# Two layers of a hybrid decoder: turning matmul results through a DRAM scratch on GpSimd's queue

## The chip, the cores and the metric

One core of one Trainium2 chip. The metric is the device time of one execution, in microseconds. Inputs are float32 and are laid out before the launch, features on the partitions.

## What is computed

Two layers on a sequence of 256 tokens with 2048 features. Every layer adds a mixer and then a gated MLP to the residual stream, each behind an RMS norm.

```
for l in range(2):
    h = rms_norm(x, mix_norm[l])
    x = x + (mixer_ab(h, ...) if l == 0 else mixer_c(h, ...))
    h = rms_norm(x, ffn_norm[l])
    x = x + conv_ffn(h, w_up[l], conv_w[l], conv_b[l], w_down[l])

conv_ffn: z = h @ w_up;  z = sum(conv_w[j] * z shifted by 2 - j tokens) + conv_b
          a, b = split(z);  return (silu(a) * b) @ w_down        # 5632 hidden
```

Mixer A is a causal gated MLP over chunks of 128 tokens, mixer B a gated linear recurrence with 8 heads, both with one output projection. Mixer C is attention with 16 heads, a forgetting gate, normalised q and k and an output gate.

## The kernel before

**Matmuls.** Each float32 weight and activation is split into a rounded part and a rest (`wh`, `wl` for weights; the two halves of a tile of 512 columns for activations), and three matmuls replace one: high by high, high by low, low by high. The weights are moved through the array in tiles of 128x1024 (two k-tiles of 128 rows by 512 output columns): a DMA on SyncE's queue (`weights`, L195), a cast on ScalarE (`wh`, L206), a subtraction on VectorE (`wl`, L211), then 12 matmuls of 512 columns. One such group is a *tick*. Buffers: four of `w` and three each of `wh` and `wl`; in the FFN every other group uses a second pool with two of each. Results stand in PSUM with tokens on the partitions, in two banks of 128 tokens; there are four banks for projections.

**Turning.** The next step needs features on the partitions. So a result of 256 tokens by 512 features, a *piece*, is evacuated by ScalarE to `z`, transposed in blocks of 32x32 by VectorE into `tmp` (`transposed`, L308), and moved to its place across partitions by DMAs (L314): 16 transfers of 32 KB per piece, eight on SyncE's queue and eight on GpSimd's. In the last piece of all, ScalarE's queue takes a share. There are 80 pieces. In the turned tile two tokens lie side by side, token t and token t + 128, and readers use a strided view (`turned`, `natural`).

**Order.** Generators hold the work around the matmuls; `tick()` advances them before each weight group. A reader of a piece begins `LAG` = 6 ticks after the piece (L315 ff. and `after`), the last piece of a layer `LAST` = 7 ticks. The tile framework then orders the instructions of each engine by its own estimate of durations, so the place of a reader in an engine's queue comes from that, with waits on semaphores where data is late.

**Pairs.** Where a layer's last pieces become the next layer's input, `project_pair` runs two accumulations at once: k-tiles 0 to 11 (`JOIN` = 12) of the first and then of the second, then tiles 12 to 15 of the first and of the second. The two pieces then end two ticks apart. The pair is used for the output projections (`output`) and at the start of each FFN.

**Other places that the change touches.** `conv` makes one ScalarE instruction and two on VectorE (L989, L990) per feature tile of 128. `forget` sends the gate row sums of mixer C to DRAM (`cd`, L806) and reads them back to all partitions in one transfer of 2 MB (`cb`, L807). `orow` is a broadcast read of 512 KB on GpSimd's queue (L541). The final pieces of the FFN go through `add_y`; the sums of its last piece (L158) stand before the sum of the last output tile (L1077) on VectorE.

Of the kernel before, what the change touches and what calls it, by code (L numbers as in the profile page):

```python
# [15 lines left out]
P = 128  # L16
# [9 lines left out]
LAG = 6  # L26
LAST = 7
WAIT = 2
JOIN = 12
EPS = 1e-6  # L30
# [23 lines left out]
def tile_trunk(ctx: ExitStack, tc: tile.TileContext, x, pp_d, cst_d, mlev_d, msk_d,  # L54
# [10 lines left out]

    count = [0]
# [18 lines left out]
    SC.dma_start(pp[:, 0:C_FFN], pp_d[:, 0:C_FFN])  # L85
# [24 lines left out]
    def turned(ap):  # L110

        return view(ap, 0, (1, 2), (2, P))

# [191 lines left out]
    def transposed(src, tmp, dst, queues=None):  # L305

        for T in range(2):
            V.transpose(tmp.rearrange("p (b m i t) -> p b m i t", b=4, m=4, t=2)[:, :, :, :, T],  # L308
                        src(T).rearrange("p (m b j) -> p b m j", m=4, b=4))
        n = 2 * BLK  # L310
        for a in range(4):
            for b in range(4):
                qs = queues or (nc.sync, nc.gpsimd)
                qs[(a + b) % len(qs)].dma_start(dst[BLK * b:BLK * (b + 1), :, a * n:(a + 1) * n],  # L314
                                  tmp[BLK * a:BLK * (a + 1), b * 4 * n:(b + 1) * 4 * n]  # L315
                                  .rearrange("p (m r) -> p m r", m=4))
# [83 lines left out]
    def add_four(q, ps, z, tmp, dst, nxt):  # L400
        for T in range(2):
            SC.activation(z[:, T], ps[T], AF.Copy)
        transposed(lambda T: z[:, T], tmp, dst)

        def rest():
            for i in range(4):
                m = 4 * q + i
                sum_in(xT[m], xT[m], dst[:, i], ALU.add)
                nxt.feed(m)
                if q < 3 or i % 2:  # L410
                    yield
            if q == 3:
                for _ in range(WAIT):
                    yield
                yield from nxt.finish_tok()

        after(LAST if q == 3 else LAG, rest())


    def mixer_ab(norm):  # L420
# [64 lines left out]
        for g in range(2):  # L485
            for T in range(2):
                i = (2 * g + T) * 4
                j = hp.tile([P, 512], F32, tag="smk", name=nm("junk"), bufs=1)
                sumsq(ss[:, i:i + 4], gv[g][:, T], j)
        rsq(ss[:, 0:2 * NH], ss[:, 0:2 * NH], P)  # L490
        for g in range(2):
            for T in range(2):
                i = (2 * g + T) * 4
                v4 = gv[g][:, T].rearrange("p (h d) -> p h d", d=P)
                V.tensor_tensor(v4, v4, ss[:, i:i + 4].unsqueeze(2).to_broadcast([P, 4, P]), ALU.mult)
# [14 lines left out]
        def mixes():  # L510
            yield
            yield
            yield
            for h in range(NH):
                mix(h)
                yield
# [21 lines left out]
        od = dp.tile([NH, P], F32, tag="od", name="od")  # L538
        orow = hp.tile([P, NH * P], F32, tag="orow", name="orow")
        nc.gpsimd.dma_start(od.rearrange("h p -> p h"), omlb)  # L540
# [3 lines left out]
        def turn(w4, late=False, use=None):  # L544
# [8 lines left out]
            t = t.rearrange("p (m t) -> p m t", m=4)  # L553
# [3 lines left out]
        def natural(z):  # L557
            return view(z, 0, (1, 2), (2, P))

        lf, kq, pair = [], [], []  # L560

        def gates(h, z):
# [5 lines left out]
            act_in(l.rearrange("p (t n) -> p t n", t=2), natural(z), AF.Sigmoid)  # L568
            act_in(t[:, 0::2], natural(z), AF.Sigmoid, scale=-1.0)
# [4 lines left out]
        def four_gates(j, z):  # L574
            for i in range(4):
                gates(4 * j + i, z[:, i])
                yield
# [6 lines left out]
        def hgrn(h):  # L584
# [68 lines left out]
            for T in range(2):  # L653
                SC.activation(itok[:, T, d0:d0 + P], op[:, T * P:(T + 1) * P], AF.Copy, scale=so[:, T:T + 1])
            left[0] -= 1

        def queries(j, z):
            while len(kq) < 4 * j + 4:
                yield
            for i in range(4):  # L660
                t = kq[4 * j + i]
                copy_in(view(t, 3 * P, (-2 * P, 2), (1, P)), natural(z[:, i]), AF.Copy)
# [33 lines left out]
        def gated(j, ps):  # L696
# [6 lines left out]
            t = hp.tile([P, 1024], F32, tag="QK", name=nm("turn"), bufs=2).rearrange("p (m t) -> p m t", m=4)  # L703
# [4 lines left out]
            gain = pp[:, C_ON:C_ON + 1]  # L708
            for i in range(4):
                y = yB[8 + 4 * j + i] = quad("yb")  # L710
                hi, lo = (y[:, c * S:(c + 1) * S].rearrange("p (t u n) -> p t u n", t=2, u=2) for c in range(2))
                copy_in(hi, view(t[:, i], 0, (2, 2), (1, 2), (4, P // 2)), AF.Copy, scale=gain)
                for u in range(2):
                    V.scalar_tensor_tensor(lo[:, :, u], view(t[:, i], u, (2, 2), (4, P // 2)), gain,
                                           hi[:, :, u].bitcast(F32), ALU.mult, ALU.subtract)
# [3 lines left out]
        def spatial(j, z):  # L719
# [3 lines left out]
            for i in range(4):  # L723
                b = 4 * j + i
                m = mg[b].rearrange("p (t n) -> p t n", t=2)
                V.tensor_tensor(m, m, natural(z[:, i]), ALU.mult)
                yB[b] = quad("ya")
                split(yB[b], mg[b], turn=True)
                yield
# [7 lines left out]
        for q, ps in enumerate(output(w_abo, yB, NH)):  # L737
# [3 lines left out]
            dst = dst.rearrange("p (m t) -> p m t", m=4)  # L741
# [5 lines left out]
    def mixer_c(norm):  # L747
# [38 lines left out]

        def forget():
# [19 lines left out]
            nc.gpsimd.dma_start(cb, cd.partition_broadcast(P))  # L807
# [9 lines left out]
        def attend(h, q, k, v, o):  # L817
# [4 lines left out]
            for j, (t, g) in enumerate(((q, gq), (k, pp[:, C_KN:C_KN + 1]))):  # L822
                copy_in(qk[:, j].rearrange("p (t n) -> p t n", t=2), turned(t[:, h % 4]), AF.Copy, scale=g)
# [45 lines left out]
        def heads(t):  # L869
            return flat(t).rearrange("p (m t) -> p m t", m=4)  # L870

        ready = [0]

        def turn(z, t):
# [10 lines left out]
            transposed(lambda T: z[:, T], flat(piece("tmp", 2)), heads(t))  # L885
# [4 lines left out]
        for g in range(CH // 4):  # L890
            qkv = []
            for j in range(3):
# [11 lines left out]
                if j < 2:  # L904
                    t = piece("turn", 4)
                    start(turn(z, t))
                    z = heads(t)
# [6 lines left out]
        def gate(q, z):  # L914
# [6 lines left out]
            t = piece("turn", 4)  # L921
            transposed(lambda T: z[:, T], flat(piece("tmp", 2)), heads(t))
# [3 lines left out]
            for i in range(4):  # L926
# [5 lines left out]
                src = view(heads(t)[:, i], 0, (2, 2), (1, 2), (4, P // 2))  # L932
                h, lo = (y[:, i_ * S:(i_ + 1) * S].rearrange("p (t u n) -> p t u n", t=2, u=2) for i_ in range(2))
# [13 lines left out]
        for q, ps in enumerate(output(w_co, yB)):  # L947
            add_four(q, ps, piece("z", 2), flat(piece("tmp", 2)), heads(piece("turn", 4)), nxt)
# [4 lines left out]
    def ffn(l, norm, last):  # L953
# [7 lines left out]
        def room():  # L961
            return (hp.tile([P, 1024], F32, tag="tmp", name=nm("tmp"), bufs=1),
                    hp.tile([P, 4, S], F32, tag="zt", name=nm("zt"), bufs=2))
# [17 lines left out]
        def conv(z, j, half):  # L981
# [6 lines left out]
            copy_in(c, z, AF.Identity, bias=pp[:, cb:cb + 1], scale=w(2))  # L988
            V.scalar_tensor_tensor(c[:, 1:], z[:, :S - 1], w(1), c[:, 1:], ALU.mult, ALU.add)  # L989
            V.scalar_tensor_tensor(c[:, 2:], z[:, :S - 2], w(0), c[:, 2:], ALU.mult, ALU.add)  # L990
            return c

        def up(j0):
# [4 lines left out]
            def gate():  # L998
                yield from ea
                for i in range(4):  # L1000
                    a = conv(za[:, i], j0 + i, 0)
# [7 lines left out]
            def fill():  # L1009
                yield from eb  # L1010
                for i in range(4):
                    b = conv(zb[:, i], HT + j0 + i, 1)
# [11 lines left out]
        def add_y(q, finish):  # L1024
# [5 lines left out]
            def rest():  # L1030
                for i in range(4):
                    m = 4 * q + i
                    r = sum_in(xT[m], xT[m], zt[:, i], ALU.add)
# [161 lines left out]
```

## Time and profile before

| | us |
|---|---|
| median of three runs | 2317.85 (2313.73 to 2318.16) |
| the profiled execution | 2317.44 |
| its span | 2315.7 |
| mean granted TensorE clock | 0.996 |

The span is one execution as the hardware profiler saw it; 1.7 us lie around it. PE is TensorE, PEld its weight loads, DVE VectorE, ACT ScalarE, POOL GpSimd, SP SyncE; SPq, ACTq and POOL's DMA lines are issues of transfers. L211 is line 211 of the kernel. In a row of the timeline stand start, length, engine, line, operation, output <- input, shapes and count, and in brackets the idle time of the engine before it with what ended it. In a group stand busy time and mean nanoseconds of one, then the idle time before. A row of the DMA issues has the count, the size of one and the median time from issue to landing.

### The profile page before, as it was taken

What the parts mean: (1) busy time and instruction counts of PE and PEld (TensorE: products, weight loads), DVE (VectorE), ACT (ScalarE), POOL (GpSimd) and SP (SyncE); (2) the same over time, 40 slices, a digit from 0 to 9 for tenths busy, and PEclk for the clock granted to TensorE, in tenths of its full rate; (3) what the DMA queues carried; (4) which work ended last, traced back from release to release, by engine and by line L of the source; (5) the groups of instructions that cost most, each with busy time, mean ns of one, the idle gap of its engine ahead of it and who ended that gap; (6) DMA issues with size and microseconds to landing.
All of it is one profiled execution on the core that took longest, in us unless ns stands there. A gap on an engine that the chain in (4) does not pass through costs nothing.

```text
span 2315.7 us, 31427 instructions
## 1 busy us (share of the span) xinstructions
PE 2292.7 (99%) x10370; PEld 1903.9 (82%) x10370; DVE 1557.9 (67%) x2369; ACT 1313.3 (57%) x1953; POOL 356.5 (15%) x661
## 2 busy tenths in 40 slices
PE   9999999999999999999989999999999999999999
PEld 7888887888888888888868888878888888888887
DVE  7788766777566657766756665657777467657666
ACT  7577655665455545654545556646655456456642
POOL 0101121122012002111211101121221022012102
PEclk9999999999999999999999999999999999999999
DMA  8755667777667657776666555767777677667765
GB/s 273 205 186 169 187 204 222 228 235 214 203 204 218 214 185 227 221 215 189 181 198 201 185 187 174 227 207 229 235 219 219 193 213 218 204 203 219 220 204 172
DMA packets 499204, 481.06 MB, mean 208 GB/s; under 512 B 116992, under 2 KB 468368, under 8 KB 498912
## 3 DMA queue, kind: packets, MB, share of 16 engines
q1 hardware_dynamic: 475344, 451.83, 62.5%
q0 software_dynamic: 21248, 23.69, 4.6%
q10 hardware_dynamic: 2448, 3.53, 0.5%
q8 instruction: 81, 1.33, 0.2%
q14 instruction: 83, 0.68, 0.1%
HBM read 434.85 MB, written 2.12 MB: 189 GB/s over the span
## 4 chain that ended last, share of the span: by engine, by line
PE 75%; DMA 2%; DVE 1%; SPq 1%; issue 0%; ACT 0%; DVEq 0%; ACTq 0%; POOLq 0%
PE pm L288 21%; PE pm L289 21%; PE pm L287 21%; PE pm L267 3%; PE pm L268 3%; PE pm L269 3%; SPq L314 1%; DMA zt<-tmp 1%; PE px L161 1%; PE px L770 1%; DMA turn<-tmp 0%; PE pm L771 0%; DVE wl L211 0%; DVE tmp L308 0%; PE px L164 0%
## 5 line engine op out<-in xcount | busy, mean ns | idle before, releaser
L211 DVE TENSOR_TENSOR wl<-w,wh 128x1024 fp32r<-128x1024 f32 (+1 forms) x812 | 986.7, 1218 | 655.6 <-ACT wh L206 650.0
L206 ACT ACTIVATE wh<-w 128x1024 fp32r<-128x1024 f32 (+1 forms) x812 | 854.6, 1054 | 796.3 <-PE pm L289 555.6
L288 PE MATMUL pm<-wl,a 128*128 128x512 f32 x1792 | 698.4, 390 | 2.9 <-DVE wl L211 2.9
L287 PE MATMUL pm<-wh,a 128*128 128x512 f32 x1792 | 701.0, 391 | 0.0
L289 PE MATMUL pm<-wh,a 128*128 128x512 f32 x1792 | 698.1, 390 | 0.0
L314 POOL DMA_DIRECT2D zt<-tmp x413 | 223.7, 549 | 1203.0 <-DVE tmp L308 1000.6
L288 PEld LDWEIGHTS pm<-wl,a 128*128 128x128 f32 x1792 | 336.8, 188 | 73.3 <-DVE wl L211 4.6
L289 PEld LDWEIGHTS pm<-wh,a 128*128 128x128 f32 x1792 | 336.6, 188 | 69.8
L287 PEld LDWEIGHTS pm<-wh,a 128*128 128x128 f32 x1792 | 336.7, 188 | 69.2
L288 PE MATMUL pm<-wl,hid 128*128 128x512 f32 x688 | 267.9, 389 | 0.0
L287 PE MATMUL pm<-wh,hid 128*128 128x512 f32 x688 | 267.9, 389 | 0.0
L289 PE MATMUL pm<-wh,hid 128*128 128x512 f32 x688 | 267.9, 389 | 0.0
L314 POOL DMA_DIRECT2D turn<-tmp x224 | 121.4, 550 | 635.3 <-DVE tmp L308 299.1
L267 PE MATMUL pm<-wh,a 128*128 128x512 f32 x464 | 184.3, 398 | 8.3 <-ACT wh L206 8.3
L268 PE MATMUL pm<-wl,a 128*128 128x512 f32 x464 | 181.9, 392 | 0.2 <-DVE wl L211 0.2
L269 PE MATMUL pm<-wh,a 128*128 128x512 f32 x464 | 181.6, 391 | 0.0
L289 PEld LDWEIGHTS pm<-wh,hid 128*128 128x128 f32 x688 | 129.2, 188 | 26.8
L287 PEld LDWEIGHTS pm<-wh,hid 128*128 128x128 f32 x688 | 129.2, 188 | 26.7
L288 PEld LDWEIGHTS pm<-wl,hid 128*128 128x128 f32 x688 | 129.2, 188 | 26.7
L155 ACT ACTIVATE conv<-zt,pp 128x256 f32<-128x256 f32 x176 | 95.6, 590 | 24.2 <-DMA zt<-tmp 23.0
L267 PEld LDWEIGHTS pm<-wh,a 128*128 128x128 f32 x464 | 87.6, 189 | 26.0 <-ACT wh L206 8.7
L308 DVE STREAM_TRANSPOSE tmp<-z 128x512 f32<-128x512 f32 x132 | 92.2, 706 | 18.4 <-ACT z L974 16.0
(217 smaller groups left out, 1935.3 us busy)
## 6 DMA issues: line engine op xcount, KB each, us to landing
w<-in_w_up SPq DMA_DIRECT2D x352, 512.0 KB, 4.5
w<-in_w_dn SPq DMA_DIRECT2D x176, 512.0 KB, 4.3
w<-in_w_cqkv SPq DMA_DIRECT2D x88, 512.0 KB, 4.3
w<-in_w_abo SPq DMA_DIRECT2D x32, 512.0 KB, 4.4
w<-in_w_cg SPq DMA_DIRECT2D x32, 512.0 KB, 4.0
w<-in_w_co SPq DMA_DIRECT2D x32, 512.0 KB, 4.0
zt<-tmp SPq DMA_DIRECT2D x414, 32.0 KB, 2.4
zt<-tmp POOLq DMA_DIRECT2D x413, 32.0 KB, 2.3
```

What stands on the lines that cost most here:

```text
L155: return behind(SC.activation(*args, **kw), "act")
L161: return behind(PE.matmul(*args, **kw), "main")
L206: deep["act"] = SC.activation(wh[:, p], w[:, p], AF.Copy)
L211: deep["sub"] = V.tensor_tensor(wl[:, p], w[:, p], wh[:, p].bitcast(F32), ALU.subtract)
L267: PE.matmul(ps[T], ah, h, start=k + i == 0, stop=False)
L268: PE.matmul(ps[T], ah, l, start=False, stop=False)
L269: deep["main"] = PE.matmul(ps[T], al, h, start=False, stop=k + i == KT - 1)
L287: PE.matmul(ps[T], ah, h, start=k + i == 0, stop=False)
L288: PE.matmul(ps[T], ah, l, start=False, stop=False)
L289: deep["mm"] = deep["main"] = PE.matmul(ps[T], al, h, start=False, stop=k + i == n - 1)
L308: V.transpose(tmp.rearrange("p (b m i t) -> p b m i t", b=4, m=4, t=2)[:, :, :, :, T], src(T).rearrange("p (m b j) -> p b m j", m=4, b=4))
L314: qs[(a + b) % len(qs)].dma_start(dst[BLK * b:BLK * (b + 1), :, a * n:(a + 1) * n], tmp[BLK * a:BLK * (a + 1), b * 4 * n:(b + 1) * 4 * n] ...
```

## The change

A turned piece goes to a DRAM scratch in four transfers of 128 KB (32 partitions, four runs of 1 KB each) and comes back in one of 512 KB (128 rows of 4 KB), all five on GpSimd's queue. The four writes of the very last piece are on SyncE's and ScalarE's queues. In the turned tile the columns of a feature tile now lie in four runs of 64 tokens, and readers use two new views. Since runs of 64 are apart, `conv` needs for each shift a second, short instruction for the tokens that reach into the run before. The readers begin `LAG` = 5 ticks after a piece. `project_pair` splits the second accumulation at `HALF` = 8. The 2 MB read of the gate rows becomes four of 512 KB, at 0, 4, 8 and 12 ticks. The first parameters are fetched on GpSimd's queue. The v norm of mixer A is spread over ticks, and the gain of mixer B's output norm is applied by VectorE at the heads, from a row in `orow`, instead of after the turning.

```diff
-LAG = 6
+LAG = 5
+HALF = 8
...
-    SC.dma_start(pp[:, 0:C_FFN], pp_d[:, 0:C_FFN])
+    nc.gpsimd.dma_start(pp[:, 0:C_FFN], pp_d[:, 0:C_FFN])
...
+    def cell(t, m):
+        return view(t, m * 2 * BLK, (S, 4), (1, 2 * BLK))
+    def halves(t, m):
+        return view(t, m * 2 * BLK, (1, 2), (S, 4), (2, BLK))
...
     def project_pair(wa, wb, acts, shift=0):
         pa, pb = banks_for(), banks_for()
-        for part in ((0, JOIN), (JOIN, KT)):
-            for w4, ps in ((wa, pa), (wb, pb)):
-                project_four(w4, acts, KT, shift=shift, ps=ps, part=part)
-                if part[1] == KT:
-                    yield ps
+        for w4, ps, part in ((wa, pa, (0, JOIN)), (wb, pb, (0, HALF)), (wa, pa, (JOIN, KT)), (wb, pb, (HALF, KT))):
+            project_four(w4, acts, KT, shift=shift, ps=ps, part=part)
+            if part[1] == KT:
+                yield ps
...
     def transposed(src, tmp, dst, queues=None):
...
-        n = 2 * BLK
+        d = dram.tile([P, 1024], F32, tag="turn", name=nm("bounce"), bufs=6)
         for a in range(4):
-            for b in range(4):
-                qs = queues or (nc.sync, nc.gpsimd)
-                qs[(a + b) % len(qs)].dma_start(dst[BLK * b:BLK * (b + 1), :, a * n:(a + 1) * n],
-                                  tmp[BLK * a:BLK * (a + 1), b * 4 * n:(b + 1) * 4 * n]
-                                  .rearrange("p (m r) -> p m r", m=4))
+            n = slice(a * S, (a + 1) * S)
+            (queues or (nc.gpsimd, nc.gpsimd))[a % 2].dma_start(
+                d[:, n].rearrange("(b j) n -> j b n", b=4),
+                tmp[BLK * a:BLK * (a + 1)].rearrange("j (b n) -> j b n", b=4))
+        nc.gpsimd.dma_start(dst, d)
...
+        def values():                  # mixer A's v norm, with a yield after each part
...
-            nc.gpsimd.dma_start(cb, cd.partition_broadcast(P))
+            for g in range(4):
+                c = slice(4 * g, 4 * g + 4)
+                after(4 * g, rows(cb[:, c], cd[c].partition_broadcast(P)))
...
-            copy_in(c, z, AF.Identity, bias=pp[:, cb:cb + 1], scale=w(2))
-            V.scalar_tensor_tensor(c[:, 1:], z[:, :S - 1], w(1), c[:, 1:], ALU.mult, ALU.add)
-            V.scalar_tensor_tensor(c[:, 2:], z[:, :S - 2], w(0), c[:, 2:], ALU.mult, ALU.add)
+            c4 = as_cell(c)
+            copy_in(c4, z, AF.Identity, bias=pp[:, cb:cb + 1], scale=w(2))
+            n = 2 * BLK
+            for d in (1, 2):
+                for to, of in ((c4[:, :, d:], z[:, :, :n - d]), (c4[:, 1:, :d], z[:, :3, n - d:])):
+                    V.scalar_tensor_tensor(to, of, w(2 - d), to, ALU.mult, ALU.add)
```

More of the change, by code (lines that the diff above doesn't have):

```diff
@@ L884, in turn @@
             yield
-            transposed(lambda T: z[:, T], flat(piece("tmp", 2)), heads(t))
+            transposed(lambda T: z[:, T], flat(piece("tmp", 2)), t)
             for _ in range(LAG):
@@ L920, in gate @@
             yield
-            t = piece("turn", 4)
-            transposed(lambda T: z[:, T], flat(piece("tmp", 2)), heads(t))
+            t = flat(piece("turn", 4))
+            transposed(lambda T: z[:, T], flat(piece("tmp", 2)), t)
             gone[0] += 1
@@ L947, in mixer_c @@
         for q, ps in enumerate(output(w_co, yB)):
-            add_four(q, ps, piece("z", 2), flat(piece("tmp", 2)), heads(piece("turn", 4)), nxt)
+            add_four(q, ps, piece("z", 2), flat(piece("tmp", 2)), flat(piece("turn", 4)), nxt)
         es.close()
```

102 lines of the change are left out of this document (53 added, 49 removed).

## The prediction

> **What bounds the kernel.** I read the page's engine line first, then busy time and clock by stages, then the timelines of the stages that lag.
>
> ```profile
> span 2315.7 us, 31427 instructions
> ...
> PE 2292.7 (99%) x10370; PEld 1903.9 (82%) x10370; DVE 1557.9 (67%) x2369; ACT 1313.3 (57%) x1953; POOL 356.5 (15%) x661
> ```
>
> TensorE is the bound. The change adds and removes no matmul, so what can be won is only time in which TensorE stands still or runs at a low clock. The view by windows shows how much that is. Its columns are the window, its length, TensorE's busy time with the number of matmuls, the granted clock, the DMA share and GB/s.
>
> ```profile
> 340.00:372.00 32.00, 29.44 (x121) 0.95 0.63 181
> 800.00:832.00 32.00, 32.00 (x143) 1.00 0.60 191
> 1178.00:1198.00 20.00, 11.69 (x39) 0.74 0.67 213
> 1550.00:1566.00 16.00, 14.12 (x54) 0.89 0.82 247
> 40.00:60.00 20.00, 18.83 (x83) 1.00 0.60 191
> ```
>
> 800:832 is a stage without a stall: 143 matmuls in 32 us, one in 0.2238 us. At that pace 340:372 lacks 22 matmuls, 4.9 us. 1550:1566 would hold 71.5 and lacks 17.5, 3.9 us. 1178:1198 would hold 89.4 and lacks 50.4, 11.3 us. Idle time alone (2.56, 1.88 and 8.31 us) is less than that, because the clock is down to 0.95, 0.89 and 0.74 too. Together the three stages lose 20.1 us. The window 40:60 lacks 6.4 matmuls, 1.4 us.
>
> The three stages have one cause. First SyncE's queue at each of them, then ScalarE at the first (start, length, line, what, how often, idle before it and its releaser):
>
> ```profile
> 338.19 11.80 SPq L314 DMA_DIRECT2D turn<-tmp  x16
> 350.10 18.71 SPq L195 DMA_DIRECT2D w<-in_w_abo  x9
> ```
> ```profile
> 1168.65 16.12 SPq L314 DMA_DIRECT2D turn<-tmp  x16
> 1184.87 9.91 SPq L195 DMA_DIRECT2D w<-in_w_cqkv  x7
> ```
> ```profile
> 1540.46 11.16 SPq L314 DMA_DIRECT2D turn<-tmp  x16
> 1551.73 10.93 SPq L195 DMA_DIRECT2D w<-in_w_co  x7
> ```
> ```profile
> 353.99 1.06 ACT L206 ACTIVATE wh<-w 128x1024 fp32r<-128x1024 f32 x1 [5.49 <-DMA w<-in_w_abo]
> ```
>
> Two pieces are turned back to back. Sixteen small transfers, half of each piece, stand on SyncE's queue and wait for their transposes, and for 11.8, 16.1 and 11.2 us no weight is fetched behind them. ScalarE's next cast waits 5.5 us for the fetch, and TensorE waits for the cast.
>
> **What leaves SyncE.** Of all the transfers of pieces on SyncE's queue two remain, at the very end. Every weight that came late in the three stages was queued behind the sixteen, so I take off the whole 20.1 us. Also, with HALF = 8 the two accumulations end four groups of weights apart instead of two, so that two pieces do not simply meet again on GpSimd's queue. What is late next is the piece itself, whose way gets longer.
>
> **What a turned piece takes.** Before, from the end of the transposes to the first reader, in a stage without a stall:
>
> ```profile
> 545.43 0.71 DVE L308 STREAM_TRANSPOSE tmp<-z 128x512 f32<-128x512 f32 x1 [0.45 <-ACT z L974]
> ```
> ```profile
> 546.43 4.34 POOL L314 DMA_DIRECT2D zt<-tmp  x8 [17.43 <-DVE tmp L308]
> ```
> ```profile
> 550.15 1.06 ACT L206 ACTIVATE wh<-w 128x1024 fp32r<-128x1024 f32 x1 [1.66 <-DMA zt<-tmp]
> 552.87 1.06 ACT L206 ACTIVATE wh<-w 128x1024 fp32r<-128x1024 f32 x1 [1.66 <-DMA zt<-tmp]
> 553.84 2.06 ACT L155 ACTIVATE conv<-zt,pp 128x256 f32<-128x256 f32 x4
> ```
>
> The transposes end at 546.14 and the reader starts at 553.84, 7.7 us later. Afterwards, no row shows a piece that goes through DRAM; it is built from its neighbours (issues by line, KB, us to landing, and GpSimd's one dependent pair of a DRAM write and read):
>
> ```profile
> zt<-tmp POOLq DMA_DIRECT2D x413, 32.0 KB, 2.3
> ...
> turn<-tmp POOLq DMA_DIRECT2D x224, 32.0 KB, 1.9
> ...
> w<-in_w_cqkv SPq DMA_DIRECT2D x16, 256.0 KB, 2.8
> ...
> orow<-od POOLq DMA_DIRECT2D x1, 512.0 KB, 6.4
> ```
> ```profile
> 1164.39 0.51 POOL L806 DMA_DIRECT2D cd<-fc  x1 [17.69 <-DVE ss L354]
> 1166.92 0.56 POOL L807 DMA_DIRECT2D cb<-cd  x1 [2.02 <-DMA cd<-fc]
> ```
>
> GpSimd's eight issues take 4.34 us, 0.54 each, and begin 0.29 us after the transposes. The fourth write is issued at 1.92. A write of 128 KB lies between the 32 KB and the 256 KB rows, 2.3 to 2.8 us; the pair shows 2.53 us from such a write's issue to the read's. So the read goes out at about 4.5. It is 128 rows of 4 KB on GpSimd's queue, as orow is: 6.4 us; a weight-sized load could be as fast as the 2.8 of half its size. The piece is there between 7.3 and 10.9 us after the transposes, and I take 10.9, from the row of the same shape and queue: 3 us longer than before.
>
> The readers have moved as well. In the changed kernel's order on ScalarE, five or six casts stand between a piece's evacuation and its first reader in the FFN where four stood; casts are 2.72 us apart, so the readers come 10.4 or 13.1 us after the transposes. The piece is at most 0.5 us late for them, and ScalarE has casts in hand: the code gives three buffers in the mixers and five in the FFN, so two or four groups of 2.72 us, less one cast (1.06 us) and one split,
>
> ```profile
> L211 DVE TENSOR_TENSOR wl<-w,wh 128x1024 fp32r<-128x1024 f32 (+1 forms) x812 | 986.7, 1218 | 655.6 <-ACT wh L206 650.0
> ```
>
> 1.22 us: 3.2 and 8.6 us. TensorE stalls only if the piece takes over 10.4 + 3.2 = 13.6 us in a mixer or 19 us in the FFN. For what still comes late I add 1.5 us, between 0 and 6.
>
> By the Trainium skill (DMA: Bandwidth & Descriptors, Anatomy of one DMA), a transfer from GpSimd takes about 2.0 us plus its bytes over 436 GB/s. As an estimate from that page the write would take 2.3 us and the read 3.2 us, the piece 7.6 us, and the 1.5 us would be nothing.
>
> **GpSimd's queue.** It blocks at each read until the writes have landed, some 2.5 us. Behind it stand only the next piece, 11 us or more later, and around 1170 us the quarters of cb. There, by the changed order, half of the k piece's writes and two quarters stand between the q piece's read and the k piece's read. The 2 MB of cb in one was
>
> ```profile
> cb<-cd POOLq DMA_DIRECT2D x1, 2048.0 KB, 10.9
> ```
>
> so two quarters add up to 5.4 us. From the q piece's transposes, done at 1168.6: its fourth write goes out at 1170.5 and has landed at 1173.3; q's read, two writes and two quarters take 5 x 0.54 us; the later of the two writes goes out near 1174.9 and lands at 1177.7; k's read lands at 1184.1, or with the quarters' 5.4 us ahead of it at 1189.5. Its reader stands behind the cast for the seventh group after v.
>
> ```profile
> 1178.87 0.69 ACT L903 ACTIVATE v<-pm,Rt 128x512 f32<-128x512 f32 x1 [0.67 <-PE pm L269]
> ```
>
> With three buffers that cast waits for the fourth group's matmuls, 4 x 2.72 us after v's evacuation: the reader comes at about 1190. This is the tightest place.
>
> GpSimd's time for an issue hardly varies, though VectorE is 67% busy beside it (min/median/max ns):
>
> ```profile
> L314 POOL DMA_DIRECT2D zt<-tmp x413: 548/549/561, 431.2 to 2305.3; - x138
> ```
>
> The Trainium skill (SBUF — State Buffer, Who interferes with whom) speaks against the change: VectorE's two-port modes lock GpSimd out of SBUF, and GpSimd's DMAs then wait for their descriptors. The trace does not show it in 413 issues (561 ns at most).
>
> **VectorE.** Each of 176 convolutions gets two short instructions, on 3 and 6 elements.
>
> ```profile
> L345 DVE TENSOR_SCALAR rm<-ss 128x8 f32<-128x8 f32 x8 | 1.3, 164 | 0.0
> ```
>
> 352 x 0.164 is 58 us more, 67% to 70% of the span. They stand between splits of weights, which wait for casts anyway; uncovered, a piece's four convolutions would cost 8 x 0.164 = 1.3 us, but the casts in hand hide that. The v norm of mixer A becomes a generator between the casts. I give it half of the loss in 40:60, 0.7 us. The first parameters move from ScalarE's to GpSimd's queue: between -0.5 and +3 us, taken as nothing.
>
> **The tail.** Here nothing hides the piece.
>
> ```profile
> 2301.50 1.31 DVE L308 STREAM_TRANSPOSE tmp<-y 128x512 f32<-128x512 f32 x2 [0.54 <-DMA out<-x]
> ...
> 2309.16 1.43 DVE L158 TENSOR_TENSOR x<-x,zt 128x256 f32<-128x256 f32 x4 [0.68 <-DMA zt<-tmp]
> 2310.50 0.42 DVE L1076 TENSOR_TENSOR x<-x,ev 128x256 f32<-128x256 f32 x1
> 2311.03 0.78 DVE L1077 TENSOR_TENSOR x<-x,pm 128x256 f32<-128x256 f32 x2
> ```
>
> Transposes end at 2302.81, the last sum at 2311.81. Changed: two writes each on SyncE and ScalarE, the second some 0.8 us in, landed after 2.3 to 2.8 us, 2306.2; the read is issued at 2306.5 and, with no weights loading, takes 4.5 us (2.8 to 6.4), 2311.0. Four sums (1.43 us), and one 0.4 us sum instead of three, end at 2313.0 us: 1.2 us later, between -0.5 and +3.1.
>
> **Sum.** -20.1 + 1.5 - 0.7 + 1.2 = -18.1 us. The profiled execution took 2317.4 us (1.7 us around its span), which becomes 2299.3; the median of the three runs is 0.4 us above it: **2299.7 us**. With the bounds (late pieces 0 to 6, tail -0.5 to +3.1, start -0.5 to +3) the forecast lies between 2294 and 2307.
>
> **Rivals.** (1) The stall moves: GpSimd's two queued pieces come late at the stage near 1180 and in part at the others, and half of the 20.1 us comes back: 2310. For it: k's 1189.5 against 1190. Against: two casts in hand. Chance 0.14. (2) The weights are late for want of DMA bandwidth, not for the queue, and nothing is gained: 2317.9. For it: 247 GB/s in 1550:1566. Against: the first fetch starts 0.1 us after the sixteen and is cast 3.9 us later. Chance 0.04. (3) Slower: the way through DRAM outlasts the cover in the mixers. It decides from 13.6 us a piece; at 15.1 us, each of the 28 pieces there (224 issues, eight a piece) costs 1.5 us, 42 us, and the kernel takes about 2342. For it: two landings in a row, and the cb row's 10.9 us if the read shares the engines badly. Against: orow's 6.4 us was measured on this very queue and shape. The lock that the Trainium skill (SBUF — State Buffer) describes would act here, by late descriptors. Chance 0.12. The forecast keeps 0.70.
>
> **The numbers.** A measurement tells about 0.2%, 4.6 us, from no change. Faster is the forecast and rival 1, 0.84; the same is rival 2, 0.04; slower is rival 3, 0.12. The range goes from 2293 to 2315: it takes in rival 1, and leaves out rivals 2 and 3 and a little of the forecast's lower end.
>
> **What would show it.** Right: 340:372 and 1550:1566 of the new trace hold about 143 and 71 matmuls at clock 1.00; SyncE's queue has no pieces between weights; the wait of 8 us before a matmul is gone; GpSimd's reads land in 3 to 6.4 us. Wrong: casts or sums that wait for a piece, followed by idle TensorE; reads above 9 us; a last sum more than 12 us after the last transposes.

## The result, and the profile after

The changed kernel takes 2419.6 us (median of four runs, 2414.16 to 2421.18); the kernel before took 2315.8 us (four runs) on the same chip. The ratio is 1.0444, 95% interval 1.0423 to 1.0466: slower by 104 us, where 18 us less was forecast. The profiled execution took 2414.2 us, the shortest of the four. The page's span and engine line, after:

```profile
span 2412.4 us, 29885 instructions
...
PE 2326.2 (96%) x10370; PEld 1918.2 (80%) x10370; DVE 1594.2 (66%) x2729; ACT 1290.4 (53%) x1937; POOL 231.8 (10%) x425
```

The span is 96.7 us longer for the same 10370 matmuls. TensorE's busy time rose by only 33.5 us; the rest is standing still. These are the windows of the prediction in the trace after; the third and fourth are moved to where the same matmuls now run. Counted by their number, those that began at 1178.2 and 1550.2 us begin at 1225.4 and 1592.2, behind a longer FFN.

```profile
340.00:372.00 32.00, 32.00 (x143) 26.49 (x142) 24.61 (x40) 20.47 (x32) 5.50 (x10) 1.00 0.79 254
800.00:832.00 32.00, 27.67 (x110) 22.35 (x109) 20.13 (x38) 12.76 (x17) 0.00 (x0) 0.89 0.52 166
1225.00:1245.00 20.00, 16.69 (x76) 13.63 (x75) 8.92 (x14) 10.21 (x16) 3.28 (x6) 1.00 0.90 336
1592.00:1608.00 16.00, 16.00 (x72) 13.26 (x71) 13.91 (x25) 11.01 (x19) 0.56 (x1) 1.00 0.70 233
```

Two of the three lagging stages now run without a gap at clock 1.00. The one of mixer C has 76 matmuls where it had 39; TensorE waits 3.3 us in it, for ScalarE's reader of a turned piece:

```profile
1241.22 0.93 ACT L172 ACTIVATE qk<-turn,pp 128x256 f32<-128x256 f32 x2 [2.93 <-DMA turn<-bounce]
```

So most of the gain was there. The reference stage 800:832, which had been perfect, lost 33 of 143 matmuls. It lies in the FFN, and a longer stretch of the first FFN, first before and then after, says how much:

```profile
400.00:1100.00 700.00, 699.27 (x3087) 579.02 (x3086) 464.30 (x620) 385.93 (x508) 104.07 (x192) 1.00 0.70 214
```

```profile
400.00:1100.00 700.00, 666.39 (x2862) 545.84 (x2861) 450.28 (x755) 359.92 (x480) 60.49 (x110) 0.98 0.67 215
```

225 matmuls fewer, at 700 us for 3087, are 51 us in the first FFN; the second FFN shows much the same. The waits of the trace after (engine, line, what it waited for, us in total, times, longest) give the chain:

```profile
POOL zt L332 <- DMA bounce<-tmp: 187.6, 34, 6.4
ACT conv L172 <- DMA zt<-bounce: 138.3, 41, 8.3
DVE conv L1011 <- ACT conv L172: 113.4, 37, 7.7
PE pm L305 <- DVE wl L228: 70.8, 33, 5.6
```

GpSimd waits for the writes, ScalarE's first convolution for the read, VectorE for ScalarE, and TensorE for a split of weights that stands in VectorE's queue behind the convolutions. One such stall by engine, from the timelines: GpSimd first, then ScalarE, VectorE and TensorE.

```profile
580.15 2.19 POOL L329 DMA_DIRECT2D bounce<-tmp  x4 [15.27 <-DVE tmp L324]
588.34 0.56 POOL L332 DMA_DIRECT2D zt<-bounce  x1 [6.00 <-DMA bounce<-tmp]
```

```profile
588.08 1.06 ACT L223 ACTIVATE wh<-w 128x1024 fp32r<-128x1024 f32 x1 [1.66 <-PE pm L306]
593.79 1.09 ACT L172 ACTIVATE conv<-zt,pp 128x256 f32<-128x256 f32 x2 [4.65 <-DMA zt<-bounce]
594.79 1.04 ACT L223 ACTIVATE wh<-w 128x1024 fp32r<-128x1024 f32 x1
```

```profile
589.17 1.23 DVE L228 TENSOR_TENSOR wl<-w,wh 128x1024 fp32r<-128x1024 f32 x1 [1.49 <-ACT wh L223]
594.43 1.54 DVE L1011 SCALAR_TENSOR_TENSOR conv<-zt,pp,conv 128x252 f32<-128x252 f32 x5 [4.03 <-ACT conv L172]
...
600.72 1.22 DVE L228 TENSOR_TENSOR wl<-w,wh 128x1024 fp32r<-128x1024 f32 x1
```

```profile
601.99 0.76 PE L305 MATMUL pm<-wl,hid 128*128 128x512 f32 x1 [2.85 <-DVE wl L228]
```

The transposes end 0.29 us before the first write, at 579.86. GpSimd waits 6.00 us behind its last write before it issues the read, and the data is used at 593.79, 13.9 us after the transposes. ScalarE could have gone on at 589.14. At 594.79 it casts the next weights at once; had VectorE split them at once too, near 595.8 to 597.1, TensorE, which worked until 599.1, would not have noticed. But from 594.43 to 600.72 VectorE does the late piece's convolutions, products and splits, 6.3 us of them, and only then the weights. TensorE stands for 2.85 us and then runs a stretch at a low clock (window 602.0 to 605.4, eight matmuls):

```profile
602.00:605.40 3.40, 3.40 (x8) 2.75 (x9) 3.40 (x5) 1.39 (x2) 0.00 (x0) 0.51 0.56 167
```

That costs another 1.7 us. Below, the *loss* of a stretch is what the intervals between starts of the projections' matmuls have above the pace of 0.2267 us (other matmuls between them are in it). Over the whole trace it is 87.8 us before and 182.1 after; the difference, 94.3 us, is nearly the whole delay of the last matmul (2311.1 to 2406.0).

### The profile page after: what moved, and what is told of

It reads as the page before. It is cut to its first block, busy times and chain, and to the rows that moved or that the text cites. A ratio compares the mean times of both kernels' runs of the same rounds, so it can differ in the third digit from the quotient of the medians.

```text
span 2412.4 us, 29885 instructions
## 1 busy us (share of the span) xinstructions
PE 2326.2 (96%) x10370; PEld 1918.2 (80%) x10370; DVE 1594.2 (66%) x2729; ACT 1290.4 (53%) x1937; POOL 231.8 (10%) x425
## 4 chain that ended last, share of the span: by engine, by line
PE 52%; DMA 22%; DVE 14%; issue 4%; ACT 4%; POOL 2%; DVEq 0%; POOLq 0%; ACTq 0%
PE pm L305 13%; PE pm L306 13%; PE pm L304 13%; DMA bounce<-tmp 9%; DMA zt<-bounce 9%; DVE conv L1011 6%; PE pm L286 3%; PE pm L285 3%; PE pm L284 3%; DVE wl L228 3%; POOL bounce L329 2%; DMA turn<-bounce 2%; ACT wh L223 2%; DVE tmp L324 2%; PE px L178 1%
## 5 line engine op out<-in xcount | busy, mean ns | idle before, releaser
L305 PE MATMUL pm<-wl,a 128*128 128x512 f32 x1792 | 709.1, 396 | 51.4 <-DVE wl L228 51.4
L305 PEld LDWEIGHTS pm<-wl,a 128*128 128x128 f32 x1792 | 341.1, 190 | 132.9 <-DVE wl L228 62.9
L304 PEld LDWEIGHTS pm<-wh,a 128*128 128x128 f32 x1792 | 341.3, 190 | 74.0 <-ACT wh L223 2.8
L306 PEld LDWEIGHTS pm<-wh,a 128*128 128x128 f32 x1792 | 341.2, 190 | 70.9
L329 POOL DMA_DIRECT2D bounce<-tmp x316 | 173.0, 554 | 1629.5 <-DVE tmp L324 1518.1
L305 PE MATMUL pm<-wl,hid 128*128 128x512 f32 x688 | 274.0, 398 | 18.2 <-DVE wl L228 18.2
L306 PE MATMUL pm<-wh,hid 128*128 128x512 f32 x688 | 272.7, 396 | 0.0
L304 PE MATMUL pm<-wh,hid 128*128 128x512 f32 x688 | 271.2, 395 | 0.0
L1011 DVE SCALAR_TENSOR_TENSOR conv<-zt,pp,conv 128x252 f32<-128x252 f32 x704 | 195.7, 347 | 113.4 <-ACT conv L172 113.4
L285 PE MATMUL pm<-wl,a 128*128 128x512 f32 x464 | 181.1, 390 | 0.0
L306 PEld LDWEIGHTS pm<-wh,hid 128*128 128x128 f32 x688 | 132.5, 193 | 27.8
L304 PEld LDWEIGHTS pm<-wh,hid 128*128 128x128 f32 x688 | 131.8, 192 | 27.9
L286 PEld LDWEIGHTS pm<-wh,a 128*128 128x128 f32 x464 | 87.1, 188 | 18.1
L285 PEld LDWEIGHTS pm<-wl,a 128*128 128x128 f32 x464 | 87.3, 188 | 17.8 <-DVE wl L228 0.2
```

The costliest lines, as they stand in the source:

```text
L285: PE.matmul(ps[T], ah, l, start=False, stop=False)
L286: deep["main"] = PE.matmul(ps[T], al, h, start=False, stop=k + i == KT - 1)
L304: PE.matmul(ps[T], ah, h, start=k + i == 0, stop=False)
L305: PE.matmul(ps[T], ah, l, start=False, stop=False)
L306: deep["mm"] = deep["main"] = PE.matmul(ps[T], al, h, start=False, stop=k + i == n - 1)
L329: (queues or (nc.gpsimd, nc.gpsimd))[a % 2].dma_start(d[:, n].rearrange("(b j) n -> j b n", b=4), tmp[BLK * a:BLK * (a + 1)].rearrange("j ...
```

## The experiments

Theory 1: a piece is later than the place that its reader has in the queues, and the reader's work then stands ahead of the weights. Rivals: the changed VectorE work itself (theory 2), and the DRAM transfers as a load on the DMA engines (theory 3).

**Readers later.** Only the distance asked for in the FFN is changed. The planner did not follow it as I expected, to some 21 us: in the trace the first reader of a piece stands six casts behind its evacuation (eight for two pieces), a median of 12.9 us after the transposes, and the last of a piece's four convolutions begins 19.6 us after them.

```diff
 # four(), empty()
-                for _ in range(LAG):
+                for _ in range(10):
                     yield
```

> The changed kernel with one edit: in the FFN the readers of a turned piece begin 10 ticks after it instead of 5 (in the planned order they move behind the next piece's evacuation, some 21 us after the transposes). Theory 1, the way through DRAM (13.4 us) ends after the place of its readers, and their work then stands in front of the next weight split: ScalarE's waits for zt (138 us) vanish, TensorE's 71 us of waits fall below 10, about 2305 us (2295 to 2320). Theory 2, the two short instructions per convolution load VectorE too much: nothing is taken away, 2390 or more. Theory 3, GpSimd's queue and the doubled DMA traffic delay the weights: 2390 or more.

Measured: 2316.7 us, ratio to the kernel before 1.0002 (0.9992 to 1.0011). 103 us are gone, although the transfers, instructions and bytes are all still there. The same stretch of the FFN and TensorE's wait:

```profile
400.00:1100.00 700.00, 700.00 (x3092) 579.69 (x3091) 478.40 (x787) 385.30 (x503) 67.30 (x123) 1.00 0.75 233
```

```profile
PE pm L305 <- DVE wl L228: 6.5, 11, 1.1
```

Theory 1 holds; theories 2 and 3 fall as causes that would act wherever the readers stand. The transfers did not land at the same times, though. On the same queue the writes now land in 3.7 us instead of 4.7,

```profile
bounce<-tmp POOLq DMA_DIRECT2D x316, 128.0 KB, 3.7
```

and the median way of a piece, from its transposes to the landing of the read, falls from 13.5 to 12.6 us. The 2305 us was missed: by the loss, the first 100 us lost 6 us more than before, 100 to 300 and 1400 to 1500 some 2 to 3 us more each, and the end behind the last matmul was 1.8 us longer. Just behind the stage near 1181, 4 us of what it had won came back.

**No scratch, all on GpSimd's queue.** Sixteen direct transfers of 32 KB a piece; everything else as changed.

```diff
-        d = dram.tile(...)            # and four writes, one read
+            for b in range(4):
+                nc.gpsimd.dma_start(dst[BLK * b:BLK * (b + 1), a * S:(a + 1) * S],
+                                    tmp[BLK * a:BLK * (a + 1), b * S:(b + 1) * S])
```

> The changed kernel without the DRAM scratch: 16 direct transfers of 32 KB per piece (1 KB runs), all on GpSimd's queue; everything else as changed. 16 issues at 0.54 us and a landing of 2.3 us make about 11 us; the planned readers stand five casts on, 10.4 us. Theory 1: late by 1 us at most, about 2305 us (2298 to 2335). Theory 2 (short instructions, still there): 2390 or more. Theory 3 in the form that GpSimd's queue is too slow for a whole piece: 2380 or more, with 16 issues even slower than five.

Measured: 2491.9 us, ratio 1.0766 (1.0750 to 1.0782). A miss of my expectation. Without DRAM the kernel became slower still. The landing is 4.5 us,

```profile
zt<-tmp POOLq DMA_DIRECT2D x821, 32.0 KB, 4.5
```

and GpSimd's issues are broken by waits for transfers issued earlier. One piece on GpSimd's queue takes from 571.3 to 582.7 only to be issued:

```profile
571.29 3.92 POOL L329 DMA_DIRECT2D zt<-tmp  x8 [13.48 <-DVE tmp L324]
578.02 0.98 POOL L329 DMA_DIRECT2D zt<-tmp  x2 [2.81 <-DMA zt<-tmp]
579.25 0.50 POOL L329 DMA_DIRECT2D zt<-tmp  x1 [0.24 <-DMA zt<-tmp]
580.27 2.45 POOL L329 DMA_DIRECT2D zt<-tmp  x5 [0.53 <-DMA zt<-tmp]
```

So it does not take DRAM to make this kernel slow; what counts is when the piece is there.

**Without the short instructions.** Left out are the 352 instructions on 3 and 6 elements; the tokens at the start of a run then lack their neighbours from the run before.

```diff
-                for to, of in ((c4[:, :, d:], z[:, :, :n - d]), (c4[:, 1:, :d], z[:, :3, n - d:])):
+                for to, of in ((c4[:, :, d:], z[:, :, :n - d]),):
```

> The changed kernel with the two short convolution instructions left out (the tokens that reach into the run before do not get their neighbours; the output is not the reference's). VectorE has 352 instructions less, some 45 us. Theory 1: the lateness stays and only the burst behind it gets 1.3 us shorter, so each of some 24 stalls loses 1.3 us and perhaps a clock window: 2370 to 2400. Theory 2: the loss goes with them, about 2310.

Measured: 2399.0 us, ratio 1.0356 (1.0339 to 1.0374). They are worth 20.6 us here; they are part of the burst behind a late piece. Where no piece is late (first experiment), they cost nothing that shows.

**The kernel before, pieces on GpSimd's queue alone.** It was to show whether SyncE's queue caused the three stalls.

```diff
-                qs = queues or (nc.sync, nc.gpsimd)
+                qs = queues or (nc.gpsimd,)
```

> The kernel before with one edit: all 16 transfers of a piece on GpSimd's queue, none on SyncE's. If the three stalls near 350, 1180 and 1555 us come from pieces standing before weights on SyncE's queue, they go: 2296 to 2310, less if pieces that take 11 us instead of 7.7 come late somewhere. If they had another cause: 2316 or more.

Measured: 2323.2 us, ratio 1.0030 (1.0018 to 1.0042); slower, not faster. The last matmul came 5 us earlier, but the end behind it took 16.9 us instead of 4.6. All three stalls went, the one near 1181 too, although the gate rows still came in one read:

```profile
1178.00:1198.00 20.00, 18.84 (x81) 14.88 (x81) 8.59 (x8) 7.38 (x8) 8.70 (x16) 1.00 0.90 284
```

Around 1117 to 1135 others came, 8 us together. So SyncE's queue without pieces is enough to remove the three stalls, and the time went elsewhere. Its landing was 4.1 us, as slow as in the second experiment, and yet the FFN lost nothing: the planner had put these readers six or seven casts behind the evacuation, or behind the next one. It had put all 44 at five in the second experiment, which lost 139 of its 175 us in the FFNs, counted over the same matmuls.

**Writes on SyncE's queue.** One edit to the changed kernel, the read stays where it is.

```diff
-            (queues or (nc.gpsimd, nc.gpsimd))[a % 2].dma_start(
+            (queues or (nc.sync, nc.sync))[a % 2].dma_start(
```

> The changed kernel with one difference: the four writes to the scratch go out on SyncE's queue, the read back stays on GpSimd's. The scratch, the sizes, the readers and everything else are those of the changed kernel. Theory A (the writes are slow because GpSimd's own queue handles them: 4.1 to 4.7 us landing there, 2.9 us for the same transfer on SyncE's queue in the last piece): the read is issued about 3 us after the last write and not 6, the way of a piece falls from 13.4 to about 10.5 us, below the reader's cover, so most of the 95 us of FFN waits go; SyncE's queue stands again in front of the weight loads at the three places of before, for up to 20 us. Time 2320 to 2350. Theory B (a write to DRAM is slow to be seen by a dependent read, whatever queue it is on): the read is issued 5.5 to 6 us after the last write as before, the FFN waits stay, 2395 to 2430.

Measured: 2314.3 us, ratio to the kernel before 0.9983 (0.9973 to 0.9992): below my range, and 105 us below the changed kernel. The rows of the DMA issues, first after, then here:

```profile
bounce<-tmp POOLq DMA_DIRECT2D x316, 128.0 KB, 4.7
zt<-bounce POOLq DMA_DIRECT2D x52, 512.0 KB, 5.4
```

```profile
bounce<-tmp SPq DMA_DIRECT2D x318, 128.0 KB, 3.1
zt<-bounce POOLq DMA_DIRECT2D x52, 512.0 KB, 4.7
```

Over the 80 pieces the median from the last write to the read is 3.7 us instead of 6.0, and from the transposes to the read 5.2 instead of 8.0. Piece by piece, the median way falls from 13.5 to 10.6 us. The planner also put 36 of the 44 FFN readers at six casts, where the changed kernel has 17 at six and 27 at five, so a part of this run's gain is place. The eight at five have a way of 10.4 us and cost TensorE nothing, so for them the shorter way was enough. The FFN runs at full pace. One stall is back, 7.7 us before 1189.1. There ScalarE waits for a turned piece of mixer C, and the next cast stands behind it:

```profile
1187.15 0.93 ACT L172 ACTIVATE qk<-turn,gq 128x256 f32<-128x256 f32 x2 [7.74 <-DMA turn<-bounce]
```

That piece's read was issued at 1180.39, 12 us after its transposes.

**The kernel before, GpSimd's queue except for the final pieces.**

```diff
-                qs = queues or (nc.sync, nc.gpsimd)
+                qs = queues or (nc.gpsimd,)
...
-                       (nc.sync, SC, nc.gpsimd) if end else None)
+                       (nc.sync, SC, nc.gpsimd) if end else (nc.sync, nc.gpsimd) if last and finish else None)
```

> The kernel before with its 16 direct transfers of a piece all on GpSimd's queue, except the pieces of the very last sums, which keep the queues that they had (SyncE's and GpSimd's). In the run with all pieces on GpSimd's queue the last matmul was 5 us earlier than in the kernel before, and the end behind it 12.4 us later. If that end is only the late final pieces, it goes back to about 4.5 us and the time is 2306 to 2312. If the end belongs to something else (the queue is full with earlier pieces), the time stays at 2320 to 2325.

Measured: 2313.9 us, ratio 0.9988 (0.9978 to 0.9997). The end behind the last matmul fell from 16.9 to 7.9 us, not to 4.6: mostly the final pieces, and a miss by 2 us.

**Later readers, direct tail, parameters on ScalarE's queue.**

```diff
 # to the first experiment's kernel
-    nc.gpsimd.dma_start(pp[:, 0:C_FFN], pp_d[:, 0:C_FFN])
+    SC.dma_start(pp[:, 0:C_FFN], pp_d[:, 0:C_FFN])
...
 # add_y of the last layer's final sums: 16 direct transfers, queues of the kernel before
```

> The changed kernel with the FFN's readers later, as in the first experiment (2316.7 us), with two more edits: the pieces of the very last sums go directly in 16 transfers on the queues of the kernel before, without the scratch, and the first parameters are fetched on ScalarE's queue as before. By the excess over the matmuls' pace the first experiment lost 6 us more than the kernel before in the first 100 us, and its end behind the last matmul was 1.8 us longer. If the parameters' queue and the tail's way are what cost it: 2308 to 2311, faster than both kernels. If the loss at the start is of another part (the spread v norm and the short gain instructions of mixer A and B): 2313 to 2316.

Measured: 2316.4 us, ratio 1.0004 (0.9991 to 1.0017). The first 100 us lost 10.1 instead of 13.4 us and the end 4.9 instead of 6.4, but 200 to 400 and 1500 to 1600 lost some 4 us more each. So neither of the two explains what the first experiment gave back; it is spread over the mixers and is not settled.

**No scratch, two queues.** As the second experiment, with SyncE's and GpSimd's queues in turn.

```diff
+        qs = queues or (nc.sync, nc.gpsimd)
```

> The changed kernel without the scratch: 16 direct transfers of 32 KB per piece on SyncE's and GpSimd's queues in turn as before, every other part of the change kept (runs of 64 tokens and the short instructions, the split at 8, four gate reads, the spread norm). The planner then puts the FFN's readers 3 casts (8.2 us) behind the piece, where the kernel before had 4. Theory 1 (the loss is the piece's way against the place that the planner gave its reader): the way on two queues is about 7 us, so it fits and the FFN shows no waits; the SyncE waits come back as in the kernel before: 2308 to 2330. Theory 2 (the readers' nearer place, or the other parts of the change, cost the FFN its time whatever the way): 2370 or more.

Measured: 2354.0 us, ratio 1.0155 (1.0136 to 1.0173), between the two. The FFN shows the same stalls, 20 instead of 33:

```profile
PE pm L305 <- DVE wl L228: 29.1, 20, 3.8
```

My 7 us for the way were wrong here: in one stall the transposes end at 480.34, the last issue ends at 487.5, and the reader gets the data at 492.8, 12.5 us later, at a place three casts behind the evacuation. A piece may be late without any DRAM, and the planner's place was nearer than the way was long.

**The two stages of writes split.** FFN writes on SyncE's queue, mixers' on GpSimd's, direct tail, parameters on ScalarE's queue.

```diff
-                transposed(lambda T: z[T], tmp, zt)
+                transposed(lambda T: z[T], tmp, zt, (nc.sync, nc.sync))
```

> The changed kernel with the four writes to the scratch on SyncE's queue in the FFN alone and on GpSimd's in the mixers, the pieces of the very last sums direct on the queues of the kernel before, and the first parameters on ScalarE's queue. The run with all writes on SyncE's queue took 2314.3 us; it showed one stall of 8 us and its half clock near 1181 us, where in the trace SyncE's queue is in front of TensorE, and none in the FFN. If that stall is SyncE's queue, putting the mixers' pieces back on GpSimd's queue takes some 11 us from the window 1100 to 1200, the tail and the start 1 to 3 us: 2300 to 2304, faster than both kernels. If the stall has another cause (the pair of the fourth mixer piece itself): 2311 to 2315.

Measured: 2323.5 us, ratio 1.0034 (1.0021 to 1.0048). A miss. I had taken the stall of the run with all writes on SyncE's queue for weights held up by that queue; its row shows a reader that waits for a turned piece. With the mixers' writes on GpSimd's queue the pair's data is still late: TensorE waits 3.7 us before 1197.2. The profiled execution, 2317.0 us, was the fastest of five, and its trace does not hold what the others lost.

**The split at 8 alone, in the kernel before.**

```diff
-        for part in ((0, JOIN), (JOIN, KT)):
-            for w4, ps in ((wa, pa), (wb, pb)):
+        for w4, ps, part in ((wa, pa, (0, JOIN)), (wb, pb, (0, 8)), (wa, pa, (JOIN, KT)), (wb, pb, (8, KT))):
```

> The kernel before with one difference: project_pair splits the second accumulation at k-tile 8 and not 12, so that its two pieces end four groups apart and not two. The prediction gave the three stalls at 352, 1181 and 1555 us wholly to SyncE's queue, which all pieces share with the weight loads. If the spacing of the pair is what takes two of them (352 and 1555; in the run with direct pieces on two queues and the split at 8 they were gone although SyncE's queue still carried pieces), the time falls by 8 to 11 us to 2305 to 2309. If only the queue matters, no change: 2314 to 2318.

Measured: 2308.3 us, ratio 0.9960 (0.9948 to 0.9973): 8.2 us faster. The three windows:

```profile
340.00:372.00 32.00, 31.68 (x140) 25.92 (x139) 24.28 (x39) 20.49 (x32) 8.60 (x16) 1.00 0.76 226
1178.00:1198.00 20.00, 12.28 (x47) 9.50 (x48) 8.23 (x16) 10.13 (x23) 1.86 (x4) 0.74 0.69 227
1550.00:1566.00 16.00, 16.00 (x72) 13.12 (x71) 12.98 (x22) 11.54 (x17) 2.79 (x6) 1.00 0.89 273
```

Two of the three stalls go while SyncE's queue still carries half of every piece. It was two pieces at once that the queue could not hide there.

**The slowest way, readers later.** The second experiment with the first one's edit.

> The second experiment (no scratch, 16 direct transfers of a piece all on GpSimd's queue, 2491.9 us) with one difference: the FFN's readers are asked for 10 ticks on, which puts them behind the next evacuation, as in the first experiment. The way stays the slowest of all tried. If the FFN's loss is the way of a piece measured against the place of its reader, all 176 us of it go although no transfer became faster: 2312 to 2335 (the end behind the last matmul stays some 10 us long, since the final pieces are late). If the loss is in the transfers themselves (they take the DMA engines from the weight loads), it stays above 2400.

Measured: 2367.0 us, ratio 1.0216 (1.0195 to 1.0237). 125 of the 175 us go with the reader's distance alone (all FFN readers stand six or eight casts on), and the FFN stretch holds 3042 matmuls, 50 short of full pace. The rest is in the mixers, whose readers were not moved (100 to 300 lost 43 us against 24 before), in FFN stalls of up to 2.9 us (some 14 us in all, over the same matmuls), and in the tail. The theory holds for most of it; my range did not count the mixers.

**Split at 8, four gate reads, mixer C on GpSimd's queue.** Three parts of the change, in the kernel before.

```diff
 # as the split at 8, and
-            nc.gpsimd.dma_start(cb, cd.partition_broadcast(P))
+            for g in range(4):
+                c = slice(4 * g, 4 * g + 4)
+                after(4 * g, rows(cb[:, c], cd[c].partition_broadcast(P)))
...
-            transposed(lambda T: z[:, T], flat(piece("tmp", 2)), heads(t))
+            transposed(lambda T: z[:, T], flat(piece("tmp", 2)), heads(t), (nc.gpsimd,))
```

> The kernel before with three parts of the change: the split at 8 in project_pair (2308.3 us alone), the gate rows in four reads at 0, 4, 8 and 12 ticks, and the pieces of mixer C's q, k and gate on GpSimd's queue alone, direct as before. In the kernel with the split alone one stall of 8.3 us, one of 2.6 and half clocks are left near 1177 to 1190; SyncE's queue there issues the 16 transfers of the q and k pieces over 15.8 us while the 2 MB read of the gate rows is in flight. In the first experiment, with four reads and no pieces on SyncE's queue, the window 1100 to 1300 lost 19.9 us of pace where the split alone loses 27.7. Expected 2298 to 2304; if the stall is of mixer C's readers and not of that queue, 2307 to 2312.

Measured: 2297.2 us (2295.2 to 2299.75), ratio 0.9912 (0.9898 to 0.9927). This is 0.8 us below the range that I expected, and beats both kernels, by 20 and by 122 us. The last large stall is gone; a wait of 1.4 us is left in its place:

```profile
1178.00:1198.00 20.00, 18.63 (x85) 15.19 (x83) 9.85 (x14) 9.89 (x16) 9.61 (x18) 1.00 0.82 275
```

The four reads of the gate rows and the emptier queue were not tried apart here. In the run with all pieces on GpSimd's queue this stall went with the gate rows in one read.

## Why the prediction was wrong

**The 20.1 us: right in size, half right in cause.** Counted over the same matmuls, the three stages gained 5.0, 13.2 and 4.1 us, and 4.9 us came back just behind the second, the one of mixer C. The pieces' place on SyncE's queue was not the one cause: taking them off it removes all three stalls, but spacing the pair alone removes two. Only the one near 1181 needs the queue to be free of pieces.

**The way of a piece: the write's landing was sized too small.** Predicted 10.9 us; median 13.5. The issues are as predicted (0.29 and 1.93) and the read's landing was put too high (6.4 forecast, 5.4 measured in the FFN). The step that failed is "2.3 to 2.8 us" for a write: the read went out 6.0 us after the last write, not 2.5 (medians over the 80 pieces, issue to issue). I took it from the rows of 32 and 256 KB and from a pair with one write of 16 KB, issued while the DMA engines were 0.49 busy (1164 to 1167). In the stall shown, four writes stood beside the weight loads, and in the 8 us of the writes the DMA engines were 0.95 busy (the column before GB/s):

```profile
580.00:588.00 8.00, 8.00 (x37) 6.64 (x36) 4.64 (x4) 3.10 (x3) 2.19 (x4) 1.00 0.95 311
```

By the Trainium skill (DMA: Bandwidth & Descriptors, Anatomy of one DMA) each write would take 2.3 us, as an estimate from its fit for one transfer; the row here says 4.7 us. The Trainium skill says in the same section that completion can take surprisingly long when the target is HBM. That agrees in sign, but the target alone does not make the 6.0 us: the same four writes to the same DRAM let the read go after 3.7 us on SyncE's queue, and after 5.2 us on GpSimd's own queue in the run with later readers. What of the 6.0 us is GpSimd's queue and what is sharing with the loads was not separated.

**The cover: the step that cost the 104 us.** The prediction said that TensorE stalls in the FFN only if a piece takes over 19 us, from the reader's place (10.4 us) and five buffers' casts in hand (8.6 us). In the stall shown the piece took 13.9 us and TensorE stood for 2.85, so about 11 us was the point from which TensorE waits: 9.3 us of place (579.86 to 589.14) and 1.8 us of cover. The place was near the forecast; the cover was not. The 8.6 us let the next weights be cast and split the moment that the data came. In fact the late piece's own work comes first in VectorE's queue, 6.3 us of it. The changed kernel's 13.5 us lie above this point, the 10.6 us with writes on SyncE's queue below, and the run with later readers moved the point itself. The term for late pieces, 1.5 us (0 to 6), came out at about 107 us in the two FFNs, counted over the same matmuls.

The other stalls say the same. Each part of the hidden features needs two pieces, a and b of the formula, and the readers of b also make the products and the splits. Of the 44 FFN pieces 27 have five casts between evacuation and first reader, and 17 have six; their ways are alike (medians 13.7 and 14.3 us). The 21 pieces b with five casts cost TensorE 64.4 us (the row of its waits above has 70.8), the six pieces a with five casts 1.7, and the 17 pieces with six nothing. With five casts and a reader that is 4 to 5 us late, a piece b costs 2.2 to 4.3 us and a piece a 0.2 to 1.2: the lateness is the same, the work ahead of the weights is not.

**VectorE's short instructions: not hidden.** The forms of the convolution's line on VectorE:

```profile
L1011 DVE SCALAR_TENSOR_TENSOR conv<-zt,pp,conv 128x6 f32<-128x6 f32 x176 | 38.7, 220 | 0.0
L1011 DVE SCALAR_TENSOR_TENSOR conv<-zt,pp,conv 128x3 f32<-128x3 f32 x176 | 38.6, 219 | 0.0
```

They take 0.22 us each and not 0.164; with them in that burst, the kernel takes 20.6 us longer. Called hidden, they were the second term that depended on the cover.

**Start, tail, GpSimd's queue.** The tail was forecast 1.2 us longer and came out 1.8 longer behind the last matmul. The start was not settled: 40:60 did not gain 0.7 us (80 matmuls, 83 before). The forecast's bounds were added up wrongly: its own terms give 2296 to 2309, not 2294 to 2307.

**The rivals.** Rival 3 had the sign and the mechanism, "the way through DRAM outlasts the cover", with 0.12; but it was placed in the mixers from 13.6 us, and priced at 42 us for 28 pieces. It acted in the FFN, which the prediction thought to be safe up to 19 us, and cost the 107 us there. Rival 1 came true in part at its tight place: k's read landed 25.5 us after q's transposes (1215.7 to 1241.2), where 20.9 was forecast, and 4.9 us of that stage's gain were lost again. Rival 2 is refuted by the gain of the three stages. The lock of VectorE on GpSimd played no part that these runs show: in the changed kernel GpSimd's issues for pieces took 0.53 to 0.57 us throughout.

## What to carry to other kernels

A wait in an engine's queue costs the lateness plus all the work of the late data that stands ahead of the next thing the bound engine needs; count that burst against the buffers, not the wait alone. When a transfer is made longer, move its reader by as much and look at where the order actually puts it: here one number in the readers' distance was worth 103 us with the same transfers, and what it did to the order was to put every first reader at least six casts on. And take a transfer's landing from a row in the same traffic, not from a quieter stage.

## What the runs showed that was not expected

A 128 KB write to the scratch landed in 4.7 us on GpSimd's queue and in 3.1 us on SyncE's, but in 3.7 us on GpSimd's when the FFN did not stall, so the queue is not the whole difference. With all sixteen 32 KB transfers of a piece on GpSimd's queue each landed in 3.8 to 4.5 us, and mostly from the ninth to the thirteenth on GpSimd waited for earlier ones before it issued more. With half of them there it was 2.3 us in the kernel before, and 3.8 us in the FFN of the run without the scratch on two queues. After the stall of 2.85 us TensorE ran for 3.4 us at half clock, so it cost 4.5; after the wait of 3.3 us near 1241 the clock stayed at 1.00.
